# Heads of a gated DeltaNet layer in one encoder kernel: separate streams for values, scans and outputs, SiLU on ScalarE, z multiplied in during the first gate

## Chip, cores, metric

One core of a Trainium2 chip runs the whole layer. The metric is the device time of one execution in microseconds (us), the median of several runs. TensorE (PE), VectorE (DVE), ScalarE (ACT), GpSimd (POOL) and SyncE (SP, which issues the DMAs here) each work through their own queue in order.

## The reference

One encoder layer over 1024 tokens and 16 meta tokens of 1024 channels, in float32. The change touches the branch with the gated delta rule and its neighbour:

```python
h = rmsnorm(h_res, norm1_w[l])
proj = h @ w_in[l]     # q k v z beta a | sc_b sc_c sc_x | gate_a gate_b
...
qkv = silu(depthwise_conv_centred(concatenate([q, k, v]), conv_w))     # 5 taps
qc = l2norm(qc) * DN_DK ** -0.5;  kc = l2norm(kc)
o_fwd = chunk_gated_delta_rule(qp, kp, vp, gp[:, :, 0], bp[:, :, 0])
o_bwd = flip(chunk_gated_delta_rule(flip(qp), flip(kp), flip(vp), ...))
o = o_fwd + o_bwd
o = o * rsqrt(mean(o * o) + RMS_EPS) * norm_w
o = o * silu(z)
...
y_a = o_dn @ w_branch_dn
y_b = (sc_b * depthwise_conv_centred(sc_c * sc_x, sc_conv_w)) @ w_branch_sc
merged = sigmoid(gate_a) * y_a + sigmoid(gate_b) * y_b
h_res = h_res + merged @ w_out
```

A SwiGLU block and a final norm follow. There are 8 heads of 128 channels; `depthwise_conv_centred` on `sc_c * sc_x` has 3 taps.

## The kernel before

Activations lie with channels on the partitions. Every float32 operand of a large matmul is split into a high and a low fp32r part, and a product is three matmuls (high x high, high x low, low x high).

**The stage of heads** (lines 200 to 1333) takes nearly half of the time. Its order is not left to the scheduler: a planner in Python emits the instructions of all engines one by one and keeps a clock `T` for each engine, advanced by estimates: `pe(ns)` for TensorE, `V(n)` for VectorE, `A(n)` or `on("act", ns)` for ScalarE. TensorE's backbone are dense units, 128 output channels each, 48 or 72 matmuls: q, k and v of each head (`u_qkv`, L366), z (`u_z`, L453), and C, x and B of the short conv (`u_short`, L417). Between two steps of a dense unit, `run_streams` (L978) resumes every stream (a generator) whose yielded time has come, and `pump` (L300) gives VectorE the next instruction of a lane: `conv`, `short`, `fs` or `norm`, the ready lane with the least weighted time spent (`WEIGHT`, L265).

The streams: `g_decay` (L508) fetches the decay rows of a head, masks them and takes their exponentials; `g_norm` (L536) makes norms and the products of keys and queries; `g_meta` (L631) does the meta tokens; `g_inv` (L649) inverts the triangular blocks, by `fs_job` on VectorE for blocks of 32 and by matmuls up to 128; `g_scan` (L751) turns the values round (L764 to 771), waits for the inverse, runs 8 steps forward and backward at once (L796 to 881), and then norms, scales, turns and stores the output (L884 to 911). In its last step it fetches z of the head (L819), which L908 multiplies in. `lock["scan"]` lets one of the inverse's matmul part and the scan at a time use the three PSUM banks of `pss()` (L67); dense units have three (`psm`, L61), `g_norm` has two (`psd`, L64).

SiLU is written as x (1 + tanh(x/2)) / 2: the factors 0.5 are in the conv weights (L1125) and the output weight (L1127), ScalarE takes the tanh (L359, L463), and VectorE multiplies (L362, L467). `half_buffer` (L344) gives the temporaries of these, of the short conv and of its products, three of them.

**The border.** Behind the stage its pools are closed (L1333) and new ones opened in the same memory. The last B unit (channels 896 to 1023 of the short conv) is loaded and multiplied there (L1437 to 1445), with `front` (L1431) loading the first operands A, E, C and so on of the next stage in between. From there on the scheduler orders the instructions. The next stage are four products of 1024 x 1024 by Strassen-Winograd, seven part products A to G each (`seven`, L1375): gate b, gate a, the short-conv branch, the DeltaNet branch. `during_gb` (L1475) lists what is put between the steps of gate b's seven products, mainly loads for gate a. The DeltaNet branch reads `o_d`, the heads' outputs in DRAM (L1541).

Of the kernel before, what the change touches and what calls it, by code (L numbers as in the profile page):

```python
# [24 lines left out]
H = 8  # L25
# [11 lines left out]
def encoder_layer(ctx: ExitStack, tc: tile.TileContext, x, meta, norm1_w, w_in,  # L37
# [29 lines left out]
    def pss():  # L67
        return ps.tile([P, 512], F32, tag="d", name=uid("pd"), bufs=3)
# [3 lines left out]
    def psany():  # L72
        rot["i"] += 1
        return (psm, psm, psm, psd, psd, pss, pss, pss)[rot["i"] % 8]()
# [137 lines left out]
    ARRIVE = 5000  # L212
    LAND = 5500
# [51 lines left out]
    WEIGHT = {"conv": 1.0, "short": 1.0, "fs": 0.33, "norm": 0.1}  # L265
# [78 lines left out]
    def half_buffer():  # L344
        return d1.tile([P, 520], F32, tag="rb", name=uid("rb"), bufs=3)

    def conv_job(raw, dst, col, st_, first):

        for h0, hn in ((first, 520 - first), HALF[1]):
# [8 lines left out]
            th = half_buffer()  # L358
            nc.scalar.activation(th[:, :hn], acc, AF.Tanh)  # L359
            on("act", 0, T["dve"] + HOP)  # L360
            yield A(hn)
            nc.vector.scalar_tensor_tensor(out=acc, in0=th[:, :hn], scalar=1.0, in1=acc, op0=ALU.add, op1=ALU.mult)  # L362
            t = V(hn, 1)
# [37 lines left out]
    def short_job(cx, j, ycs):  # L401
        for i in range(2):
            yc = half_buffer()
            ycs.append(yc)
            nc.vector.tensor_scalar(out=yc[:, :512], in0=cx[:, 1 + 512 * i:513 + 512 * i], scalar1=cols[:, j:j + 1],
                                    scalar2=None, op0=ALU.mult)
            V(512, 2)
            yield T["dve"] + DEP
# [8 lines left out]
    def u_short(j, i, w):  # L417
# [22 lines left out]
        else:  # L440
            force(st_["job"])
            ycs = [half_buffer()[:, :512] for _ in range(2)]
# [10 lines left out]
    def u_z(h, w):  # L453

        rest = None
        for i in range(2):
            po = psm()
            for k, _ in enumerate(dense_steps(po, w, hx, META + 512 * i, 512)):
                if k == 3 and rest:
                    rest()  # L460
                yield
            th = half_buffer()[:, :512]
            nc.scalar.activation(th, po, AF.Tanh, scale=0.5)  # L463
            A(512)

            def rest(i=i, th=th, po=po):
                nc.vector.scalar_tensor_tensor(out=th, in0=th, scalar=1.0, in1=po, op0=ALU.add, op1=ALU.mult)  # L467
                V(512)
                nc.sync.dma_start(z_d[h][:, 512 * i:512 * i + 512], th)
        T["dve"] = max(T["dve"], T["act"] + HOP)  # L470
        rest()
# [36 lines left out]
    def g_decay(h, st_):  # L508
# [8 lines left out]

        arrived = []
        for i in range(NC + 1):
            while i < NC and h > 1 and heads[h - 2]["steps"] <= i:  # L520
                yield T["pe"] + 100
            if i < NC:
                arrived.append(fetch(i))
            for k in ((i - 1,) if i < NC else (NC - 1,)):
                if k < 0:
                    continue
                yield arrived[k]
                nc.vector.tensor_tensor(out=PQ[:, k], in0=PQ[:, k], in1=mask2, op=ALU.add)  # L528
                yield V(256)
                for d, c in enumerate((k, NC - 1 - k)):  # L530
                    hd = d * 8 + h
                    nc.scalar.activation(PQ[:, k, d], PQ[:, k, d], AF.Exp, bias=negG2[:, c, hd:hd + 1])  # L532
                    st_["exp"][c, d] = on("act", 295)
                yield T["act"]

    def g_norm(h, st_):  # L536
# [3 lines left out]
        small = dn.tile([P, 9, 12], F32, tag="small", name=uid("small"), bufs=3)  # L540
        st_["small"] = small
        ssk, ssq, rk2, ssk1, y, _, sk = (small[:, :, i] for i in range(7))
        cc, ce = small[:, :, 7:9], small[:, :, 9:11]
# [105 lines left out]
    def g_inv(h, st_):  # L649

        NP = st_["NP"]
        E = dn.tile([P, 2, NC, 32], F32, tag="T2", name=uid("E"))
# [10 lines left out]
        for b in range(4):  # L663
            nc.scalar.copy(E[B(b)].rearrange("p d c i -> p c d i"), NP[B(b), :, :, B(b)])
            A(512)
# [23 lines left out]
        T2 = dn.tile([P, 2, NC, 32], F32, tag="T2", name=uid("T2"))[:, 0]  # L689
        rows_, turned_ = (W, Z), (Z, W)  # L690

        def diag(d, b):
            nc.scalar.copy(NP[B(b), :, d, B(b)], rows_[d][B(b), d])
            A(256)
# [635 lines left out]
    for g in rest:  # L1330
        for _ in g:
            pass
# [617 lines left out]
```

## Time and profile before

| | us |
|---|---|
| median of 3 runs | 1993.39 (1990.38 to 1996.84) |
| profiled execution | 1995.63 |
| its span, first to last instruction | 1993.9 |

Busy shares of the span, from the page: TensorE 98%, VectorE 74%, ScalarE 47%, GpSimd 9%. Stages in the profiled execution: the inputs are normed and turned round up to about 50 us; the stage of heads lasts to 941 us; the four branch products to about 1260 us; the output projection and the SwiGLU block to the end.

A row of busy times by stretch gives the stretch, its length, busy time and number of instructions of each engine, TensorE's granted clock (1.00 is full), the DMA engines' busy share and GB/s. A row of a group gives line, engine, operation, output and inputs, shapes, count, then busy time, mean ns of one, idle time before them and what ended it. A row of waits gives who waited for whom: total us, times, longest. A row of DMA issues ends with the median us from issue to landing. In a timeline row stand start and length in us. `pm`, `pe` and `pd` are the PSUM tiles of `psm`, `psd` and `pss`; `SPq` is SyncE issuing a DMA.

### The profile page before, as it was taken

The page shows a single profiled execution, that of the slowest core. Times are in us where ns is not written, and L with a number is a line of the kernel's source. Part 1 is how long each engine was busy: PE and PEld are TensorE (multiplying, and loading weights), DVE is VectorE, ACT ScalarE, POOL GpSimd, SP SyncE. Part 2 cuts the span into 40 slices and gives each one's busy share as a digit, 9 for nine tenths or more (in the row PEclk, how much of TensorE's full clock was granted, in tenths as well). Part 3 has the DMA queues.
Part 4 walks back from the last instruction along what each step waited for, and adds up shares of the span by engine and source line. Part 5 has one row for each costly group of instructions (what it writes and reads, how often), then busy time and mean ns, then how long its engine had stood idle before and what let it go on. Part 6 is the DMA issues. An engine that isn't in the chain of part 4 may idle for free.

```text
span 1993.9 us, 32160 instructions
## 1 busy us (share of the span) xinstructions
PE 1945.6 (98%) x11914; PEld 1700.9 (85%) x11914; DVE 1479.4 (74%) x2812; ACT 937.0 (47%) x2142; POOL 173.5 (9%) x497
## 2 busy tenths in 40 slices
PE   9999999999999999998999999999999999999998
PEld 8998899898989899987788788887888888888887
DVE  4788768788878788866656888758887977856574
ACT  5465475746475646342445555234323322324343
POOL 2132012123012022100000000000000000000001
PEclk9999999999999999999999999999999999999999
DMA  4123231212222112254864732332575645487654
GB/s 143 53 62 86 77 89 38 80 42 68 59 70 52 57 49 70 70 166 151 322 226 144 263 127 84 118 121 68 191 237 201 227 152 185 154 282 247 190 181 160
DMA packets 218226, 267.37 MB, mean 134 GB/s; under 512 B 14756, under 2 KB 133957, under 8 KB 216661
## 3 DMA queue, kind: packets, MB, share of 16 engines
q1 hardware_dynamic: 218069, 265.33, 41.0%
q8 instruction: 93, 1.52, 0.3%
q14 instruction: 64, 0.52, 0.1%
HBM read 192.84 MB, written 72.43 MB: 133 GB/s over the span
## 4 chain that ended last, share of the span: by engine, by line
PE 58%; DVE 4%; ACT 2%; DMA 1%; issue 1%; POOL 0%; POOLq 0%; SPq 0%; ACTq 0%; DVEq 0%
PE pm L331 6%; PE pm L1390 5%; PE pd L1390 5%; PE pe L1390 4%; PE pm L1676 3%; PE pm L1677 3%; PE pm L1675 3%; PE pd L1675 2%; PE pd L1677 2%; PE pd L1676 2%; PE pe L1675 2%; PE pe L1676 2%; PE pe L1677 2%; PE pm L1833 1%; PE pm L1834 1%; PE pm L1832 1%
## 5 line engine op out<-in xcount | busy, mean ns | idle before, releaser
L331 PE MATMUL pm<-hTh,wh 128*128 128x384 f32 (+4 forms) x1200 | 433.9, 363 | 0.1
L331 PE MATMUL pm<-hTh,wl 128*128 128x384 f32 (+4 forms) x1200 | 402.2, 336 | 0.0
L331 PE MATMUL pm<-al,wh 128*128 128x384 f32 (+4 forms) x1200 | 401.0, 335 | 0.5 <-DVE al L1057 0.5
L331 PEld LDWEIGHTS pm<-hTh,wh 128*128 128x128 f32 x1200 | 227.1, 190 | 9.2 <-ACT hTh L1051 0.2
L331 PEld LDWEIGHTS pm<-hTh,wl 128*128 128x128 f32 x1200 | 226.1, 189 | 10.3
L331 PEld LDWEIGHTS pm<-al,wh 128*128 128x128 f32 x1200 | 227.3, 190 | 8.4 <-DVE al L1057 0.7
L86 DVE TENSOR_TENSOR al<-raw,ring_h 128x1024 fp32r<-128x1024 f32 x73 | 88.4, 1222 | 64.3 <-ACT ring_h L85 64.1
L85 ACT CAST ring_h<-raw 128x1024 fp32r<-128x1024 f32 x73 | 77.0, 1055 | 109.7 <-PE pd L1834 38.0
L947 DVE TENSOR_TENSOR wl<-raw,wh 128x512 fp32r<-128x512 f32 x106 | 72.5, 685 | 43.2 <-ACT wh L950 43.0
L354 DVE SCALAR_TENSOR_TENSOR kq<-ra,wc,kq 128x520 f32<-128x520 f32 (+1 forms) x128 | 95.7, 748 | 1.5
L85 ACT CAST raw<-pair 128x1024 fp32r<-128x1024 f32 (+1 forms) x56 | 53.8, 961 | 86.7 <-PE pd L1390 34.9
L127 POOL TENSOR_SCALAR ss<-ss 128x1 f32<-128x1 f32 x13 | 4.5, 349 | 1015.5 <-ACT b L1844 602.5
L86 DVE TENSOR_TENSOR wl<-pair,wh 128x1024 fp32r<-128x1024 f32 (+1 forms) x56 | 61.9, 1106 | 39.5 <-ACT wh L85 39.4
L86 DVE TENSOR_TENSOR raw<-pair,raw 128x1024 fp32r<-128x1024 f32 (+1 forms) x56 | 61.9, 1105 | 29.8 <-ACT raw L85 27.8
L85 ACT CAST wh<-pair 128x1024 fp32r<-128x1024 f32 (+1 forms) x56 | 53.8, 960 | 61.0 <-PE pe L1390 29.0
L828 ACT ACTIVATE w<-pd,small 128x128 f32<-128x128 f32 x128 | 40.0, 364 | 88.6 <-PE pd L821 72.8
L485 DVE TENSOR_TENSOR tm<-fP,fN 128x126 f32<-128x126 f32 (+22 forms) x248 | 62.9, 254 | 6.9
L489 DVE TENSOR_TENSOR fP<-fP,tm 128x126 f32<-128x126 f32 (+22 forms) x248 | 62.7, 253 | 6.7
L950 ACT CAST wh<-raw 128x512 fp32r<-128x512 f32 x106 | 65.2, 619 | 0.1
L1345 DVE TENSOR_TENSOR b<-pm,b 128x512 f32<-128x512 f32 x65 | 43.6, 684 | 21.7 <-PE pm L1677 19.0
L85 ACT CAST mB<-raw 128x1024 fp32r<-128x1024 f32 x24 | 25.1, 1052 | 69.8 <-DVE raw L140 53.6
L532 ACT ACTIVATE PQ<-PQ,negG 128x128 f32<-128x128 f32 x128 | 44.2, 394 | 26.4 <-DVE PQ L528 26.1
(646 smaller groups left out, 5243.6 us busy)
## 6 DMA issues: line engine op xcount, KB each, us to landing
raw<-in_w_in_dram SPq DMA_DIRECT2D x56, 512.0 KB, 4.5
raw<-in_w_gate_up_dram SPq DMA_DIRECT2D x44, 512.0 KB, 5.2
sums<-in_w_down_dram SPq DMA_DIRECT2D x22, 512.0 KB, 4.9
t_d<-sums SPq DMA_DIRECT2D x11, 1024.0 KB, 3.9
raw<-s_d SPq DMA_DIRECT2D x44, 256.0 KB, 3.4
raw<-t_d SPq DMA_DIRECT2D x44, 256.0 KB, 3.6
act_d<-b SPq DMA_DIRECT2D x43, 256.0 KB, 2.7
pair<-in_w_in_dram SPq DMA_DIRECT2D x10, 1024.0 KB, 9.8
```

What stands on the lines that cost most here:

```text
L85: nc.scalar.copy(hi, src)
L86: nc.vector.tensor_tensor(out=lo, in0=src, in1=hi.bitcast(F32), op=ALU.subtract)
L331: mm(po[:, :n], (wl if j == 2 else wh)[:, k], xl[k][:, t0:t0 + n] if j == 1 else xh[k][:, t0:t0 + n], start=(i == 0), stop=(i == 3 * KT - 1))
L354: nc.vector.scalar_tensor_tensor(out=acc, in0=raw[:, h0 + t:h0 + t + hn], scalar=wc[:, t, col:col + 1], in1=acc, op0=ALU.mult, op1=ALU.add)
L485: nc.vector.tensor_tensor(out=tv, in0=fP[:, 0:r, j:j + 1].broadcast_to([P, r, n]), in1=fN[:, j:j + 1, j + 1:32].broadcast_to([P, r, n]), o ...
L489: nc.vector.tensor_tensor(out=fP[:, 0:r, j + 1:32], in0=fP[:, 0:r, j + 1:32], in1=tv, op=ALU.subtract)
L947: nc.vector.tensor_tensor(out=u[1][1][:, k], in0=u[2][:, k], in1=u[1][0][:, k].bitcast(F32), op=ALU.subtract)
L950: nc.scalar.copy(u[1][0][:, k], u[2][:, k])
L1390: mm(bank[t], a[:, c], b, start=fresh, stop=first and k == 3 and j == 2, skip_group_check=not first)
L1675: mm(po, ah[:, k], bhk, start=k == 0, stop=False)
L1676: mm(po, ah[:, k], blk, start=False, stop=False)
L1677: mm(po, al[:, k], bhk, start=False, stop=k == 3)
```

## The change

- `g_scan` is divided: `g_vals` turns round the values, in three groups, each as soon as the scan before is past the chunks that it overwrites (`vS` is one tile for all heads now); `g_scan` holds the steps alone and no lock; `g_out` norms, scales, turns and stores. A scan starts when values, inverse and meta part are there; each kind is a stream of its own.
- PSUM: `pss` has two banks, for the scan alone; a new `psv` has one, shared under the lock by values, inverse and outputs. The inverse takes `E` and `px` from the dense banks.
- SiLU is an activation: in place in the convs, on z straight from PSUM; the factors 0.5 go. The first tap of the short conv and the output's weight go from VectorE to ScalarE.
- z is no longer multiplied in by the scan. `times_z` loads `o_d` and `z_d` of a head, multiplies and stores `o_d`, once per head in gate b's products B to E, with one buffer `w2`.
- `g_decay` takes the exponentials in batches (all 8 chunks for heads 0 and 1, else 6 and 2), and the planner counts a `LOAD` of 1283 ns on each side. Other estimates change (415, 375, 628 ns), and the weight of the lane `fs` goes from 0.33 to 4.0.
- Buffers: one `half_buffer` and one `conv_buffer` in place of three; two of `o`.
- Border: the last B unit's weights are loaded and split in the stage (`cover`), and `front`'s first entry (A and E) is issued ahead of `yc`.

```diff
     def pss():
-        return ps.tile([P, 512], F32, tag="d", name=uid("pd"), bufs=3)
+        return ps.tile([P, 512], F32, tag="d", name=uid("pd"), bufs=2)
+
+    def psv():
+        return ps.tile([P, 512], F32, tag="v", name=uid("pv"), bufs=1)
...
-    WEIGHT = {"conv": 1.0, "short": 1.0, "fs": 0.33, "norm": 0.1}
+    WEIGHT = {"conv": 1.0, "short": 1.0, "fs": 4.0, "norm": 0.1}
...
     def half_buffer():
-        return d1.tile([P, 520], F32, tag="rb", name=uid("rb"), bufs=3)
+        return d1.tile([P, 512], F32, tag="rb", name=uid("rb"), bufs=1)
+
+    def conv_buffer():
+        return d1.tile([P, 512], F32, tag="yb", name=uid("yb"), bufs=1)
...
-            th = half_buffer()
-            nc.scalar.activation(th[:, :hn], acc, AF.Tanh)
+            nc.scalar.activation(acc, acc, AF.Silu)
             on("act", 0, T["dve"] + HOP)
-            yield A(hn)
-            nc.vector.scalar_tensor_tensor(out=acc, in0=th[:, :hn], scalar=1.0, in1=acc, op0=ALU.add, op1=ALU.mult)
-            t = V(hn, 1)
+            t = A(hn)
...
         for i in range(2):
-            yc = half_buffer()
+            yc = conv_buffer()
             ycs.append(yc)
-            nc.vector.tensor_scalar(out=yc[:, :512], in0=cx[:, 1 + 512 * i:513 + 512 * i], scalar1=cols[:, j:j + 1],
-                                    scalar2=None, op0=ALU.mult)
-            V(512, 2)
-            yield T["dve"] + DEP
+            nc.scalar.activation(yc[:, :512], cx[:, 1 + 512 * i:513 + 512 * i], AF.Copy, scale=cols[:, j:j + 1])
+            yield A(512)
...
             th = half_buffer()[:, :512]
-            nc.scalar.activation(th, po, AF.Tanh, scale=0.5)
+            nc.scalar.activation(th, po, AF.Silu)
             A(512)
-
-            def rest(i=i, th=th, po=po):
-                nc.vector.scalar_tensor_tensor(out=th, in0=th, scalar=1.0, in1=po, op0=ALU.add, op1=ALU.mult)
-                V(512)
-                nc.sync.dma_start(z_d[h][:, 512 * i:512 * i + 512], th)
+            nc.sync.dma_start(z_d[h][:, 512 * i:512 * i + 512], th)
...
+        for i0, i1 in ((0, 6), (6, 8)) if h > 1 else ((0, 8),):
+            for i in range(i0, i1):
+                while h > 1 and heads[h - 2]["steps"] <= i:
+                    yield T["pe"] + 100
                 arrived.append(fetch(i))
+                if i - 2 >= i0:
+                    masked(i - 2)
+            for i in (i1 - 2, i1 - 1):
+                yield arrived[i]
+                masked(i)
+            yield T["dve"] + HOP
+            on("act", LOAD)
+            for i in range(i0, i1):
+                for d, c in enumerate((i, NC - 1 - i)):
                     hd = d * 8 + h
+                    nc.scalar.activation(PQ[:, i, d], PQ[:, i, d], AF.Exp, bias=negG2[:, c, hd:hd + 1])
                     st_["exp"][c, d] = on("act", 295)
+            on("act", LOAD)
+            yield T["act"]
...
+    def g_vals(h, st_):
+
+        vT, sk = st_["vT"], st_["small"][:, :, 5]
+        for grp, free in (((8, 3, 4), 5), ((2, 5, 1), 7), ((6, 0, 7), 8)):
+            while h and heads[h - 1].get("steps", 0) < free:
+                yield T["pe"] + 100
+            yield from take("vals")
+            pt = vbank()
             for i, c in enumerate(grp):
                 transpose(pt[:, i], vT[:, 0:P] if c == 8 else vT[:, cs(c)])
             yield pe(330)
             for i, c in enumerate(grp):
                 nc.scalar.activation(vS[:, c], pt[:, i], AF.Copy, scale=sk[:, c:c + 1])
                 A(P)
+            lock["scan"] = None
+            yield T["act"] + HOP
...
+    def g_out(h, st_):
...
             yield t
+            yield from take("out")
+            pt = vbank()
             for c in range(4):
                 transpose(pt[:, c], oacc[4 * c4 + c])
             yield pe(430)
-            nc.vector.scalar_tensor_tensor(out=oT, in0=pt, scalar=cols[:, 24:25], in1=zT[:, 4 * c4:4 * c4 + 4],
-                                           op0=ALU.mult, op1=ALU.mult)
-            V(512, 1)
+            nc.scalar.activation(oT, pt, AF.Copy, scale=cols[:, 24:25])
+            t = A(512)
+            lock["scan"] = None
...
-        if h < H and not scans and heads[h].get("sk") and "tv" in heads[h] and heads[h]["tv"]():
-            scans.append([g_scan(h, heads[h]), T["dve"] + HOP, h])
+        if h < H and not scans and all(heads[h].get(k) for k in ("inverted", "learned", "valued")):
+            scans.append([g_scan(h, heads[h]), T["pe"], h])
...
-            for q in (scans, invs, metas, norms, decs):
+            for q in (scans, vals, invs, metas, outs, norms, decs):
...
-    w = wload(w_in, OSB + 7 * P)
+    front.pop(0)()
     yc = s4(SEQ)
     nc.sync.dma_start(yc, yc_d[7])
     for i in range(2):
         po = psany()
-        dense(po, w, hx, C0 + META + 512 * i, 512)
+        dense(po, cover[1], hx, C0 + META + 512 * i, 512)
...
+    def times_z(j):
+        o_ = big("w2", [P, D], F32)
+        nc.sync.dma_start(o_, o_d[j])
+        for h_ in halves:
+            z_ = tp.tile([P, 512], F32, tag="t2", name=uid("t2"), bufs=2)
+            nc.sync.dma_start(z_, z_d[j][:, h_])
+            nc.vector.tensor_tensor(out=o_[:, h_], in0=o_[:, h_], in1=z_, op=ALU.mult)
+        nc.sync.dma_start(o_d[j], o_)
...
+    for j in range(H):
+        during_gb[1 + j // 2][2 + 2 * (j % 2)].append(lambda j=j: times_z(j))
```

More of the change, by code (lines that the diff above doesn't have):

```diff
@@ L212, in encoder_layer @@
     ARRIVE = 5000
+    LOAD = 1283
     LAND = 5500
@@ L771, in g_scan, with newbank @@
                 A(P)
-        lock["scan"] = None
-        yield T["act"] + HOP - 1000
-        while not (st_.get("inverted") and st_.get("learned")):
-            yield T["pe"] + 100
-        yield from take("scan")
+            lock["scan"] = None
+            yield T["act"] + HOP
+    def g_scan(h, st_):
+        nonlocal freed, near
+        kq, small, kn, NP, PQ = (st_[k] for k in ("kq", "small", "kn", "NP", "PQ"))
+        kT, qT = kq[:, 0], kq[:, 1]
+        cc, ce = small[:, :, 6:8], small[:, :, 8:10]
+        sso = small[:, :, 10]
+        st_["steps"] = 0
+        def newbank():
+            return pss().rearrange("p (a n) -> p a n", a=4)
         Pm = st_["Pm"]
-        O = dn.tile([P, NC, P], F32, tag="o", name=uid("o"))
+        O = st_["O"] = dn.tile([P, NC, P], F32, tag="o", name=uid("o"), bufs=2)
         oacc = [O[:, c] for c in range(NC)]
@@ L881, in g_scan @@
             yield t
+    def g_out(h, st_):
+        nonlocal scaled_heads
+        small, O = st_["small"], st_["O"]
+        ssq, y, sso = (small[:, :, i] for i in (1, 4, 10))
+        oacc = [O[:, c] for c in range(NC)]
         def norm():
@@ L890, in norm @@
             yield T["dve"] + DEP
-        lock["scan"] = None
         yield T["act"] + HOP
@@ L976, in start_streams @@
                 rest.append(block_sums())
+        h = nout
+        if h < H and not outs and heads[h].get("scanned"):
+            outs.append([g_out(h, heads[h]), T["pe"], h])
+            nout += 1
     def run_streams():
@@ L988, in run_streams @@
                         h = q.pop(0)[2]
-                        if q is scans:
-                            done += 1
-                        elif q is not decs:
-                            heads[h]["inverted" if q is invs else "learned" if q is metas else "normed"] = True
+                        done += q is outs
+                        for q_, what in ((scans, "scanned"), (vals, "valued"), (invs, "inverted"), (metas, "learned"), (norms, "normed")):
+                            if q is q_:
+                                heads[h][what] = True
                     else:
@@ L1037, in turned @@
             for g in range(2):
-                bank = banks[t, g] = (psd() if g and t < 2 else pss()).rearrange("p (k t) -> p k t", k=4)
+                third = psd if g and t < 2 else (pss, pss, psv)[turns["i"] % 3]
+                turns["i"] += third is not psd
+                bank = banks[t, g] = third().rearrange("p (k t) -> p k t", k=4)
                 for k in range(4):
@@ L1332, in encoder_layer @@
             pass
+    for k in range(cover[3][0], 4):
+        split_part(cover, k)
     ph1.close()
```

108 lines of the change are left out of this document (43 added, 65 removed).

## The prediction

> **What bounds the kernel now.** I read the page first, then the busy times by stretch, then TensorE's waits in the stage of heads, then the border behind that stage in order of time.
>
> ```profile
> span 1993.9 us, 32160 instructions
> PE 1945.6 (98%) x11914; PEld 1700.9 (85%) x11914; DVE 1479.4 (74%) x2812; ACT 937.0 (47%) x2142; POOL 173.5 (9%) x497
> core 0: us, PE busy (x) PEld busy (x) DVE busy (x) ACT busy (x) POOL busy (x), PEclk, DMA share, GB/s
> 50.00:900.00 850.00, 825.00 (x6787) 769.71 (x6786) 668.05 (x1768) 488.35 (x1516) 142.14 (x432) 1.00 0.25 71
> 941.40:949.90 8.50, 0.03 (x1) 0.01 (x1) 1.33 (x3) 0.69 (x2) 0.00 (x0) 0.75 0.82 294
> 949.90:956.00 6.10, 6.07 (x15) 4.76 (x16) 6.10 (x8) 1.49 (x3) 0.00 (x0) 0.51 1.05 390
> 956.00:1110.00 154.00, 152.76 (x670) 124.93 (x669) 99.75 (x106) 79.76 (x112) 0.00 (x0) 1.00 0.65 228
> 1110.00:1950.00 840.00, 838.99 (x3733) 693.95 (x3732) 629.08 (x808) 308.40 (x378) 7.40 (x16) 1.00 0.53 177
> ```
>
> TensorE bounds it: 98% busy, and from 956 to 1950 only 1.24 + 1.01 us are idle. The change takes away no matmul, so it can win only where TensorE stands or runs slowly: 25.0 us idle in the stage of heads (850 minus 825.00), 8.5 us at the border, and behind the border 6.1 us at a granted clock of 0.51, worth 6.1 x 0.49 = 3.0 us. That is 36.5 us in all, 1.8% of the time; small gaps after a change from small to large matmuls are not counted and stay.
>
> ```profile
> PE pe L588 <- DVE PQ L626: 8.2, 6, 2.8
> PE pd L821 <- DVE r L813: 4.2, 5, 1.2
> PE pe L82 <- DVE Nm L571: 2.9, 4, 1.4
> PE pe L82 <- ACT jk L550: 2.5, 2, 2.3
> PE pd L710 <- ACT T L704: 2.0, 2, 1.3
> PE pd L699 <- DVE W L684: 1.6, 3, 0.9
> ```
>
> These are TensorE's waits between 50 and 900 us (total, times, longest). VectorE ends 16.9 us of these 21.4. No single wait is longer than 2.8 us: the planner's order is nearly right, and what is left are many short stalls, mostly where VectorE (668 of 850 us, 79%) is late.
>
> ```profile
> 939.03 1.46 SPq L911 DMA_DIRECT2D o_d<-o  x2
> 940.82 0.39 PE L119 MATMUL pm<-al,wh 128*128 128x512 f32 x1
> 941.04 0.39 PE L120 MATMUL pm<-hTh,wl 128*128 128x512 f32 x1
> 942.25 0.32 SPq L1439 DMA_DIRECT2D s<-yc_d  x1
> 942.62 2.78 SPq L1354 DMA_DIRECT2D pair<-in_w_in_dram  x4
> 949.21 0.62 ACT L85 CAST raw<-pair 128x512 fp32r<-128x512 f32 x1 [10.36 <-DMA pair<-in_w_in_dram]
> 949.93 0.77 PE L1390 MATMUL pm<-hTh,raw 128*128 128x512 f32 x1 [8.50 <-ACT raw L85]
> ```
>
> At the border the last output leaves at 939.03, the new pools' first transfers start at 942.25 behind it, the first block lands 6.6 us after its issue (942.62 to 949.21), and TensorE has run out of work at 941.
>
> **The change part by part.**
>
> *Border.* The last short-conv unit (48 matmuls of 512 columns, one per 0.22 us by the two rows at 940.82 and 941.04: 10.6 us) is no longer loaded behind the stage; its weights are split in it. The loads of A and E go ahead of that of yc. In before this unit already ran, but between the last steps of the last scan. How much comes back depends on who ends the stage. If head 7's output does, as now, little changes: A no longer queues behind the load of yc (942.25 to 942.62, 0.4 us). If dense units end it, the unit's 10.6 us lie over the 6.6 us of the load, and idle time and slow clock go: 11.5 us.
>
> ```profile
> L784 PE MATMUL pd<-vS,meta_inv x16: 270/273/275, 206.1 to 875.4; 128*128 128x128 f32 x16
> L885 DVE TENSOR_SCALAR small<-small x8: 151/164/168, 273.2 to 933.7; 128x9 f32<-128x9 f32 x8
> ```
>
> L784 opens each of the 8 scans and L885 follows it: a scan starts every (875.4 - 206.1)/7 = 95.6 us and lasts 58 us (875.4 to 933.7) to 67 us (206.1 to 273.2). About a third of the cycle no scan runs, because the inverse takes the lock only after the scan has let go of it. With own banks for the scan, inverse h+1 can lie beside scan h, the heads finish earlier, and dense work is left for the end. I take 9 of 11.5 us, ends 0 and 11.5.
>
> *VectorE to ScalarE.*
>
> ```profile
> L362 DVE SCALAR_TENSOR_TENSOR kq<-rb,kq 128x520 f32<-128x520 f32 (+1 forms) x32 | 22.1, 690 | 9.4 <-ACT rb L359 9.4
> L362 DVE SCALAR_TENSOR_TENSOR vT<-rb,vT 128x520 f32<-128x520 f32 x16 | 11.2, 698 | 8.9 <-ACT rb L359 8.8
> L467 DVE SCALAR_TENSOR_TENSOR rb<-rb,pm 128x512 f32<-128x512 f32 x16 | 10.9, 678 | 5.2 <-ACT rb L463 5.1
> L405 DVE TENSOR_SCALAR rb<-ra,cols 128x512 f32<-128x512 f32 x16 | 7.7, 480 | 3.3 <-DMA p_d<-rb 3.3
> L908 DVE SCALAR_TENSOR_TENSOR o<-pd,cols,vS 128x512 f32<-128x512 f32 x16 | 11.9, 742 | 7.9 <-PE pd L82 7.7
> L463 ACT ACTIVATE rb<-pm 128x512 f32<-128x512 f32 x16 | 9.5, 593 | 13.4 <-PE pm L331 13.3
> L532 ACT ACTIVATE PQ<-PQ,negG 128x128 f32<-128x128 f32 x128 | 44.2, 394 | 26.4 <-DVE PQ L528 26.1
> L1690 ACT ACTIVATE b<-b x21: 626/634/635, 1364.3 to 1764.9; 128x512 f32<-128x512 f32 x21
> L1690 ACT ACT_TABLE_LOAD  x1: 1283/1283/1283, 1363.0 to 1363.0; - x1
> ```
>
> All five VectorE groups go from the stage: 22.1 + 11.2 + 10.9 + 7.7 + 11.9 = 63.8 us, so VectorE falls from 79% to 71%. ScalarE keeps its activations (SiLU in place of tanh) and gains 16 short-conv products and 16 outputs, 32 x 0.593 = 19 us. It also gains table loads: SiLU needed one at L1690, where tanh, exp, square and copy had run without. Each batch of exponentials now stands between two loads: 2 batches for heads 0 and 1, 2 x 6 for the others, 14 x 2 x 1.283 = 36 us, and a few at the gates. ScalarE goes from 488 to about 545 us of 850, 64%: room on average. I take 10 of the 25.0 us of waits as won, ends 0 and 22 (the small waits on the first rows do not all belong to VectorE's load).
>
> By the Trainium skill, "ScalarE: Activation LUTs", section "What ACT_TABLE_LOAD costs", a switch costs 1.28 us of load and 1.38 us of drain, which speaks against this part. The load in this trace is 1.283 us, and the skill's drain does not show there: L1690 loads at 1363.0 and activates at 1364.3. With the drain the 28 loads would be an estimated 39 us dearer, still hidden on average.
>
> *What the bursts cost.* ScalarE is taken for 16 x 0.394 + 2 x 1.283 = 8.9 us at a stretch for heads 0 and 1, 7.3 us (12 exponentials) and 4.1 us (4) for the others. Behind a burst stand the copies out of the dense banks, the halves of the next weights and the scan's w and v2. The three dense banks give two chunks of time; a chunk is 24 matmuls of 347 columns on average (1040 in three chunks), so 2 x 24 x 0.22 x 347/512 = 7 us, less when the inverse borrows one for E or px. The trace has no such burst, so bounds: 0, if all fits; 14 x 2 us = 28 us, if each burst overruns by 2.
>
> ```profile
> yc_d<-rb SPq DMA_DIRECT2D x16, 256.0 KB, 2.2
> SPq L515 <- PE pd L841: 251.2, 45, 13.8
> ```
>
> The buffers shrink too: one conv buffer for both halves of a short-conv row makes ScalarE, in order, wait for the first half's store before it starts the second, 0.3 + 2.2 us, 8 times, 20 us of standing ScalarE, more where the SP queue waits for a scan (the second row). The scan has two banks in place of three: its second bank is rewritten (L806) right after L803, so the output adds of the step before (L875) are now due then. I take 5 us for bursts, buffers and banks together, ends 0 and 48; nearest to nothing, since the average load stays under two thirds.
>
> *z later.* 8 calls times_z in products B to E of the first gate: each loads 1 MB, multiplies twice 0.68 us (as L467), stores 0.5 MB; the fetch of z in the scan goes (0.5 MB each).
>
> ```profile
> pair<-in_w_in_dram SPq DMA_DIRECT2D x10, 1024.0 KB, 9.8
> pair<-o_d SPq DMA_DIRECT2D x4, 256.0 KB, 2.8
> tb_d<-s SPq DMA_DIRECT2D x16, 256.0 KB, 2.2
> 942.00:975.00 33.00, 25.07 (x98) 20.48 (x99) 20.27 (x23) 10.89 (x17) 0.00 (x0) 0.84 0.95 350
> 975.00:1000.00 25.00, 25.00 (x112) 20.67 (x112) 17.08 (x17) 15.35 (x21) 0.00 (x0) 1.00 0.67 231
> ```
>
> VectorE has room for 10.9 us more (17.08 of 25). DMA is full (0.95) until 975, and behind it a third is free. I take 1 us, ends 0 and 57 (worked out as the third rival).
>
> *Sum* against the profiled execution, 1995.6 us (span 1993.9): - 9 - 10 + 5 + 1 = -13, 1982.6. The median of the runs, 1993.4, lies 2.2 us under the profiled one, so 1980 us.
>
> **The rivals.**
>
> 1. *The scans no longer wait, and TensorE is full.* Inverses beside scans let dense work run unbroken at the end. For it: the 95.6 us cycle around a 60 us scan. Against: TensorE works now through the whole cycle, so there is nothing to win but the 25.0 us. Border 11.5 and 20 of the waits, costs 2: 1993.4 - 29.5 = 1964.
>
> 2. *It does not do what it says: the waits change owner.* The short stalls come from an order fixed ahead that no planner gets quite right, now with ScalarE in bursts. Border 9, waits 10, costs 17: 1993.4 - 2 = 1991.
>
> 3. *Slower, through times_z's one buffer.* The loads of call j+1 wait until call j is stored, and the multiply stands in VectorE's queue ahead of the operand splits and the sums that TensorE waits for. A cycle is load, 2 x 0.68, store: with the rows of small transfers 2.8 + 1.4 + 2.2 = 6.4 us, with the crowded 1 MB row 9.8 + 1.4 + 2.2 = 13.4. The calls lie two to a product, 48 x 0.22 = 10.6 us, so 8 calls have 42 us and some three operand steps of lead, 8 us; it decides from (42 + 8)/8 = 6.3 us a cycle. At 13.4 it costs 107 - 50 = 57 us, at a middle 9.5 us 26. Against it: if the scheduler puts the multiplies late in VectorE's queue, nothing waits, since o_d is not read before the last branch. With 26 us on the forecast: 2006.
>
> **How the numbers follow.** Forecast 1980 (1972 to 1988): 0.42. Rival 1, 1964: 0.20. Rival 2, 1991: 0.20. Rival 3, 2006 and beyond: 0.18. About 0.3% (6 us) can be told from no change: faster 0.60, same 0.22, slower 0.18. The range from 1955 (all of 36.5 us and a little) to 2006 leaves out the further part of rival 3 and little else.
>
> **What would show it.** Border: TensorE's gap between its last dense matmul and the first at L1390 under 2 us, granted clock there near 1.00. VectorE: about 604 us between 50 and 900, and the waits of L588 and L821 on it halved. ScalarE: some 30 table loads of 1.283 us, and TensorE's new waits, if any, with ScalarE or a dense bank as releaser. Scan banks: waits of L806 on L875. times_z: no wait of L1390 on VectorE, no VectorE wait for o_d or z. The forecast is wrong if the idle time of the stage stays at 25 us or more, if head 7's output still ends the stage, or if TensorE stands in the first gate.

## The result, and the profile after

The changed kernel takes 2010.75 us (median of 4 runs, 2005.81 to 2011.42), the kernel before, beside it, 1993.99 (1990.38 to 1996.84): a ratio of 1.008, 95% interval 1.0057 to 1.0103. It is slower; 1980 us with a range of 1955 to 2006 was forecast, so the time lies outside the range, on the wrong side. The profiled execution took 2011.1 us, its span 2009.4 against 1993.9.

First the page of the changed kernel:

```profile
span 2009.4 us, 32113 instructions
PE 1951.0 (97%) x11914; PEld 1707.5 (85%) x11914; DVE 1423.4 (71%) x2733; ACT 984.2 (49%) x2198; POOL 164.7 (8%) x497
```

Then its busy times by stretch (columns as before):

```profile
50.00:900.00 850.00, 809.44 (x6734) 760.14 (x6734) 618.96 (x1705) 541.04 (x1598) 132.89 (x432) 0.98 0.22 63
...
900.00:950.00 50.00, 50.00 (x227) 41.41 (x226) 13.20 (x25) 9.61 (x23) 2.18 (x1) 1.00 0.46 151
950.00:1000.00 50.00, 50.00 (x222) 41.20 (x221) 30.59 (x34) 20.25 (x29) 0.00 (x0) 1.00 0.81 296
1000.00:1050.00 50.00, 49.47 (x219) 40.63 (x218) 33.17 (x42) 24.13 (x37) 0.00 (x0) 1.00 0.92 313
1050.00:1100.00 50.00, 50.00 (x222) 41.42 (x221) 28.60 (x33) 24.71 (x35) 0.00 (x0) 1.00 0.93 325
1100.00:1150.00 50.00, 45.64 (x189) 35.97 (x189) 42.91 (x45) 24.45 (x30) 0.00 (x0) 0.97 0.78 271
```

Three stages tell three stories. The border is clean: no idle time and full clock from 900 to 1000, where before had 8.5 us idle and 6.1 us at clock 0.51. The stage of heads is worse: 40.6 us idle (850 minus 809.44) against 25.0, and a granted clock of 0.98 against 1.00. And the first gates, between 1100 and 1150, now stand 4.4 us, behind DMA engines at 0.92 and 0.93.

How much each is worth shows one group of matmuls that both kernels have in the branch products, first and last start. The first row is of the kernel before, the second of the changed one:

```profile
L1390 PE MATMUL pm<-raw,raw x132: 389/389/390, 974.8 to 1245.5; 128*128 128x512 f32 x132
```

```profile
L1413 PE MATMUL pm<-raw,raw x132: 387/389/497, 984.3 to 1260.7; 128*128 128x512 f32 x132
```

By their first start 984.3 - 974.8 = 9.5 us are lost, by their last 15.2: so the branch products lose 5.7 us. With the border's 11.5 us won (8.5 + 3.0, the prediction's own count), the stage of heads must have lost some 21 us (9.5 + 11.5).

TensorE's waits in the changed kernel between 50 and 900 us (total, times, longest):

```profile
PE pe L587 <- DVE PQ L625: 15.1, 9, 2.9
PE pe L587 <- DVE fP L481: 9.2, 3, 3.6
PE pd L822 <- DVE r L817: 4.6, 2, 2.7
```

The second of these rows in the kernel before (the first stands in the prediction):

```profile
PE pe L588 <- DVE fP L489: 0.7, 1, 0.7
```

VectorE's waits between 50 and 850, first of the kernel before, then of the changed one:

```profile
DVE wl L947 <- ACT wh L950: 37.4, 27, 7.8
```

```profile
DVE wl L955 <- ACT wh L958: 65.7, 28, 10.9
...
DVE vT L361 <- ACT vT L392: 13.4, 9, 3.0
DVE kq L361 <- ACT kq L392: 13.0, 10, 2.1
```

L587 (L588 before) multiplies keys and queries into the two `psd` banks, and VectorE reads them out (L619, L625). The waits of L588 on VectorE were to be halved; they went from 8.9 us (8.2 + 0.7) to 24.3 (15.1 + 9.2), with VectorE 49 us less busy; those of L821 (now L822) stayed, 4.2 and 4.6. VectorE is late because it stands, mostly in front of L955, which subtracts the high part of the next weights once ScalarE has rounded it (L958), and also in front of L361, the taps of the convolution that add to the one ScalarE makes (L392). Ten waits at L587 are longer than 1 us: in the trace five of them, 14.6 us, follow a stand of VectorE at L955, four, 7.6 us, one at L361. One place of the changed kernel in order of time shows how (start, length, idle time before and its releaser):

```profile
355.20 1.28 ACT L530 ACT_TABLE_LOAD   x1
...
356.49 3.62 ACT L530 ACTIVATE PQ<-PQ,negG 128x128 f32<-128x128 f32 x12
...
360.02 0.60 ACT L958 CAST wh<-raw 128x512 fp32r<-128x512 f32 x1
...
360.66 0.69 DVE L955 TENSOR_TENSOR wl<-raw,wh 128x512 fp32r<-128x512 f32 x1 [4.66 <-ACT wh L958]
...
363.56 0.60 DVE L619 SCALAR_TENSOR_TENSOR NP<-pe,small,PQ 128x128 f32<-128x128 f32 x2
...
364.38 0.41 DVE L625 TENSOR_TENSOR PQ<-pe,PQ 128x256 f32<-128x256 f32 x1
...
364.94 0.87 PE L587 MATMUL pe<-kq 128*128 128x256 f32 x2 [3.63 <-DVE fP L481]
```

A load and twelve exponentials hold ScalarE for 4.9 us. The high part waits behind them; VectorE, whose queue is in order, stands 4.66 us in front of the low part; the reads of the banks stand behind that; and TensorE, out of work at 361.3, goes on at 364.94, after 3.63 us. The releaser named in the last row is another instruction of the same late queue; what frees the bank is L625.

The wait is paid for twice. The same place of the changed kernel, by stretch:

```profile
361.00:365.00 4.00, 0.37 (x4) 0.13 (x2) 3.72 (x16) 3.27 (x9) 0.42 (x2) 1.00 0.00 0
365.00:368.00 3.00, 3.00 (x13) 2.89 (x13) 2.63 (x6) 0.00 (x0) 2.24 (x9) 0.55 0.02 5
368.00:371.00 3.00, 2.32 (x73) 1.96 (x71) 2.82 (x11) 2.34 (x9) 1.26 (x3) 0.88 0.27 43
```

After the 3.63 us TensorE is busy, but at a granted clock of 0.55 for 3 us, then 0.88: 3 x 0.45 + 3 x 0.12 = 1.7 us more.

### The profile page after: what moved, and what is told of

Same layout as the page of the kernel before. It is cut to its first block, busy times and chain, and to the rows that moved or that the text cites. A ratio compares the mean times of both kernels' runs of the same rounds, so it can differ in the third digit from the quotient of the medians.

```text
span 2009.4 us, 32113 instructions
## 1 busy us (share of the span) xinstructions
PE 1951.0 (97%) x11914; PEld 1707.5 (85%) x11914; DVE 1423.4 (71%) x2733; ACT 984.2 (49%) x2198; POOL 164.7 (8%) x497
## 4 chain that ended last, share of the span: by engine, by line
PE 79%; DVE 8%; ACT 7%; DMA 4%; issue 2%; SPq 0%; POOL 0%; POOLq 0%; DVEq 0%; ACTq 0%
PE pm L335 24%; PE pm L1413 4%; PE pm L1710 3%; PE pe L1413 3%; PE pm L1711 3%; PE pm L1709 2%; PE pd L1413 2%; PE pe L1710 2%; PE pd L1710 2%; PE pe L1711 2%; PE pe L1709 2%; PE pd L1709 2%; PE pd L1711 2%; PE pm L1868 1%; PE pm L1867 1%
## 5 line engine op out<-in xcount | busy, mean ns | idle before, releaser
L955 DVE TENSOR_TENSOR wl<-raw,wh 128x512 fp32r<-128x512 f32 x108 | 74.0, 686 | 77.8 <-ACT wh L958 77.6
L361 DVE SCALAR_TENSOR_TENSOR kq<-ra,wc,kq 128x520 f32<-128x520 f32 (+1 forms) x128 | 95.7, 748 | 14.4 <-ACT kq L392 13.0
L958 ACT CAST wh<-raw 128x512 fp32r<-128x512 f32 x108 | 66.4, 619 | 23.5 <-PE pm L335 23.3
L132 POOL TENSOR_TENSOR small<-small,minus_half 128x9 f32<-128x9 f32 x16 | 30.6, 1910 | 406.0 <-DVE small L592 255.7
L587 PE MATMUL pe<-kq 128*128 128x256 f32 x128 | 38.7, 403 | 24.3 <-DVE PQ L625 15.1
L1368 DVE TENSOR_TENSOR b<-pm,b 128x512 f32<-128x512 f32 x65 | 43.6, 684 | 24.6 <-PE pm L1711 22.2
```

What stands on the lines that cost most here:

```text
L361: nc.vector.scalar_tensor_tensor(out=acc, in0=raw[:, h0 + t:h0 + t + hn], scalar=wc[:, t, col:col + 1], in1=acc, op0=ALU.mult, op1=ALU.add)
L955: nc.vector.tensor_tensor(out=u[1][1][:, k], in0=u[2][:, k], in1=u[1][0][:, k].bitcast(F32), op=ALU.subtract)
L958: nc.scalar.copy(u[1][0][:, k], u[2][:, k])
```

## The experiments

Five theories were tested: **A**, the transfers of `times_z` cost the gates some 5 us. **B**, ScalarE in bursts makes VectorE stand at the weights' low part, and TensorE pays. **C**, the rival: streams, banks and overlap of inverse and scan are at fault, and a repair at the low part only reshuffles the waits. **D**, the border was forecast right. **E**, the weight of the `fs` lane. Changes in us are between medians, against the changed kernel unless another run is named; "before" was run again with each group of experiments, at 1994.3 to 1995.2.

**1. No `times_z`** (z is not multiplied in).

```diff
-    for j in range(H):
-        during_gb[1 + j // 2][2 + 2 * (j % 2)].append(lambda j=j: times_z(j))
```

> Leaves out the multiplication by silu(z) (the eight calls of times_z with their loads and stores). Theory A (the 4 MB of extra transfers keep the DMA engines at .92 in 1000 to 1100 and so the pieces of in_w and the first products of the gates come late): 4 to 7 us less than the changed kernel, about 2005 us, and no wait of PE over 1 us behind an input weight in 1050 to 1150. Rival (the weights would be late there anyway, since cover and border were moved): within 2 us of the changed kernel, with that wait of PE still there. The stage of heads (50 to 900) must look as in the changed kernel in both cases: about 40 us of idle PE.

2005.64 us, 5.1 less; the ratio to before is 1.0056 (1.0041 to 1.0071). TensorE's wait behind an input weight goes, and DMA shares fall to 0.70 and 0.49 between 1000 and 1100; the stage of heads is as before this edit. Theory A holds.

**2. High parts first, low parts when due.**

```diff
+        i = (0, 2, 1, 3)[i]
...
-            if ahead[0] and n_ in SPL:
-                split_part(ahead[0], SPL.index(n_))
+            if ahead[0]:
+                i_ = ahead[0][3][0]
+                if i_ < 4 and n_ >= SPL[i_] and (i_ < 2 or max(T["pe"], T["dve"]) >= ahead[0][3][i_ - 1]):
+                    split_part(ahead[0], i_)
```

(`split_part` also records in `ahead[0][3]` when the planner takes a high part for ready.)

> Only the order changes: both parts of the high weights are issued on ScalarE first, and the parts that VectorE subtracts are issued only once the planner takes the high part for ready. Theory B (a batch of exponentials holds ScalarE some 5 us, VectorE stands in front of the subtraction behind it, and the copies of the kkq banks queue behind that): VectorE's waits for the high part fall from 65.7 us to under 30 in 50 to 850, PE's idle time in 50 to 900 from 40.6 to about 30, the time by 8 to 12 us to about 2000 us. Theory C (what is lost is lost at the split of the streams and the banks, which this doesn't touch): VectorE's waits for the high part fall too, but others of VectorE grow instead, and the time stays within 3 us of the changed kernel.

1998.27 us, 12.5 less. VectorE's waits for the high part fall from 65.7 to 3.6 us; others grow (for L807 15.9 to 26.3), as C has it, but the time falls as B has it, and TensorE is idle 33.8 us in place of 40.6. VectorE still stands behind ScalarE's bursts, now at the tap, and TensorE's waits at L587 fall only to 13.1 us:

```profile
268.85 0.76 DVE L361 SCALAR_TENSOR_TENSOR vT<-ra,wc,vT 128x520 f32<-128x520 f32 x1 [4.61 <-ACT vT L392]
...
270.09 1.20 PE L587 MATMUL pe<-kq 128*128 128x256 f32 x2 [4.56 <-DVE PQ L625]
```

**3 and 4. No table loads; then no batches either** (tanh in place of SiLU in the stage of heads, so z, q, k and v differ from the reference's).

```diff
-    LOAD = 1283
+    LOAD = 0
...
-            nc.scalar.activation(acc, acc, AF.Silu)
+            nc.scalar.activation(acc, acc, AF.Tanh)
...
-            nc.scalar.activation(th, po, AF.Silu)
+            nc.scalar.activation(th, po, AF.Tanh)
```

The second one also has the loop of the kernel before in `g_decay`: two exponentials at a time.

> Computes tanh where the stage of heads computes SiLU (convolutions and z), so that ScalarE loads no table there, and the planner counts none; the exponentials stay in their batches. Theory B1 (the loads make the burst): PE's idle time in 50 to 900 falls from 40.6 to about 28, the time by 10 to 15 us to about 1998. Theory B2 (the twelve exponentials together make it: 3.6 us of them against 1.3 us of load): a fall of 2 to 6 us, to about 2006. Theory C (split and banks): within 3 us of the changed kernel.

> As the kernel with tanh in place of SiLU in the stage of heads, and the exponentials are issued two at a time between other work, as in the kernel before, not in batches of twelve and four. Theory B1: as with the batches, about 1998 us. Theory B2: PE's idle time in 50 to 900 falls to about 25, the time by 12 to 18 us to about 1995. Theory C: still within 3 us of the changed kernel, with VectorE's waits for the high part back at about 37 us and PE's waits for the kkq banks nevertheless over 15 us.

2001.85 us, 8.9 less, and 1993.64 us, 17.1 less. So loads and batches cost about alike, 8.9 and 8.2 us. Both sizes of B were partly right, and C is out as the only cause. TensorE's waits for VectorE at L587 fall to 3.0 us and then 1.4 (L580 there), though VectorE still stands some 41 us in front of the low part in both. But even the second only equals before, although the border is won and VectorE has 46 us less to do: something is left, of which `times_z` is some 5 us.

**5. The border alone**, in the kernel before.

```diff
+    fill_units.append((OSB + 7 * P, None, None, None))
...
-    w = wload(w_in, OSB + 7 * P)
+    front.pop(0)()
     yc = s4(SEQ)
...
-        dense(po, w, hx, C0 + META + 512 * i, 512)
+        dense(po, cover[1], hx, C0 + META + 512 * i, 512)
```

> The kernel before with the border of the change alone: the eighth cover's weights are loaded and split in the stage of heads, and the first entry of front is issued ahead of yc. Theory D (the border was forecast right, and the loss is all in the stage and the gates): 9 to 13 us less than before, 1981 to 1986 us, no gap of PE over 2 us in 935 to 960, VectorE's waits and PE's 25 us of idle time in 50 to 900 as before. Rival (in the kernel before the last head's scan and output end the stage, so a cover split early has nothing to hide and the slow clock stays): at most 3 us less, 1991 us or more.

1992.14 us, ratio 0.9991 (0.9983 to 1.0000): theory D falls, the rival holds. SyncE's queue of this kernel, then TensorE at the border:

```profile
936.32 1.47 SPq L911 DMA_DIRECT2D o_d<-o  x2
939.53 0.93 SPq L1360 DMA_DIRECT2D pair<-in_w_in_dram  x2
...
945.59 0.77 PE L1396 MATMUL pm<-hTh,raw 128*128 128x512 f32 x1 [7.09 <-ACT raw L85]
```

The first weights of the gates are issued behind the store of head 7's output, as before, and land as late. The gap of 8.5 us shrinks to 7.1. What freed the border in the changed kernel is the earlier end of the heads. Its scans open with the first row, its outputs are stored with the second; the third is the store of the kernel before:

```profile
L788 PE MATMUL pd<-vS,meta_inv x16: 270/275/275, 217.6 to 836.3; 128*128 128x128 f32 x16
...
L917 SPq DMA_DIRECT2D o_d<-o x16: 319/320/376, 300.8 to 914.7; - x16
...
L911 SPq DMA_DIRECT2D o_d<-o x16: 319/320/381, 281.0 to 940.2; - x16
```

A scan starts every (836.3 - 217.6)/7 = 88.4 us in place of 95.6, the last output leaves at 914.7 in place of 940.2, and dense units end the stage.

**6. As 4, with the order of 2.**

> As the kernel with tanh in place of SiLU and the exponentials spread out, and both high parts of the weights are issued first, VectorE's subtractions once the high part is taken for ready. Theory B (the 41 us that VectorE still stands in front of the subtraction there pass through to PE): 5 to 8 us less than that kernel, 1986 to 1989 us, PE's idle time in 50 to 900 under 20. Theory C (a plan is only reshuffled; other waits grow): within 3 us of it, PE's idle time still about 25.

1973.03 us, ratio 0.9896 (0.9882 to 0.991): 20.6 less than 4, where 5 to 8 were expected. Its stage by stretch:

```profile
50.00:900.00 850.00, 836.54 (x6895) 783.55 (x6894) 622.64 (x1721) 518.97 (x1594) 144.69 (x433) 1.00 0.25 70
```

TensorE is idle 13.5 us, and the clock is whole. This is what was left in 4: the low part at the head of VectorE's queue costs more than batches or loads alone. Against the changed kernel the two repairs together give 37.7 us, more than the 17.1 of 4 and the 12.5 of 2 added up.

**7. As 4, the weight of `fs` as before the change.**

```diff
-    WEIGHT = {"conv": 1.0, "short": 1.0, "fs": 4.0, "norm": 0.1}
+    WEIGHT = {"conv": 1.0, "short": 1.0, "fs": 0.33, "norm": 0.1}
```

> As the kernel with tanh in place of SiLU and the exponentials spread out, with the weight of the fs jobs back at 0.33. Theory E (at weight 4.0 the fs jobs go to VectorE ahead of the copies that free banks): 3 to 7 us less than that kernel, 1987 to 1991 us. Rival (the weight decides nothing): within 3 us of it, 1991 to 1997 us; at the low weight the inverse may also start later, which would show as PE waits for fP.

2003.61 us, 10.0 more than 4. Theory E falls: the new weight helps.

**8. As 2, z multiplied in where the DeltaNet branch reads `o_d`**, on GpSimd.

```diff
             nc.sync.dma_start(dn_[key][:, k, hi], o_d[4 * kh + k][:, halves[half]])
+        w_ = big("w2", [P, 2, 512], F32)
+        zs = [w_[:, 0], w_[:, 1]] + [tp.tile([P, 512], F32, tag="t2", name=uid("t2"), bufs=2) for _ in range(2)]
+        for k in range(4):
+            nc.sync.dma_start(zs[k], z_d[4 * kh + k][:, halves[half]])
+        for k in range(4):
+            x_ = dn_[key][:, k, hi]
+            nc.gpsimd.tensor_tensor(out=x_, in0=x_, in1=zs[k], op=ALU.mult)
```

> The kernel with the weights' high parts first, and without times_z: z is multiplied in where the last product's blocks of o are read, 16 pieces on GpSimd, so o is neither read nor written once more (4 MB of transfers in place of 12). Theory A (the transfers of times_z cost the gates 5 us, and GpSimd is idle where it now multiplies): 4 to 6 us less than with the high parts first alone, about 1993 us, DMA share at most .7 in 1000 to 1100. Rival (GpSimd's multiplications come late and the sums of the last product's blocks wait for them): the time stays at 1998 us or above, with VectorE or PE waiting for a pair behind GpSimd in 1100 to 1250.

2004.31 us, 6.0 more than 2. The gates are rid of their wait (DMA share 0.68 and 0.48 between 1000 and 1100), but a new one appears in the branch behind them:

```profile
1150.00:1200.00 50.00, 44.68 (x185) 36.37 (x184) 44.97 (x48) 18.55 (x21) 6.97 (x4) 0.93 0.42 138
```

TensorE stands 5.3 us between 1150 and 1200, with VectorE busy 45 of 50 us; VectorE waited 2.8 us for a weight of the DeltaNet branch. The DMA share between 1100 and 1150 is 0.82, against 0.76 in 2. A multiplication takes GpSimd 1.8 to 2.0 us, against 0.68 on VectorE. How much is GpSimd's slowness and how much the transfers' new place was not told apart.

**9. The order of 2 alone, in the kernel before.**

> The kernel before with nothing but the order of the weights' parts changed: both high parts first on ScalarE, VectorE's subtractions once the high part is taken for ready. Theory B (VectorE standing in front of that subtraction is a loss of every version of this stage, 37 us of it in the kernel before): 6 to 12 us less than before, 1982 to 1988 us, PE's idle time in 50 to 900 under 20. Rival (it only matters where scans, inverses and outputs may run apart, as in the change): within 3 us of before, PE's idle time about 25.

1985.74 us, ratio 0.9955 (0.9939 to 0.9972), 9.5 less. VectorE's waits for the high part fall from 37.4 to 2.6 us, TensorE's idle time in the stage from 25.0 to 20.3, and the gap at the border from 8.5 to 3.6, since the heads end earlier here too. So the loss is older than the change. By VectorE's waits (37.4 and 65.7 us) the change made it larger; the gains, 9.5 and 12.5 us, lie too close to show that.

**10 and 11. SiLU from tanh as before, exponentials spread, the order of 2; then z in the output, too.** Nothing is left out. The tanh goes into the row buffer that the taps have read already:

```diff
-            nc.scalar.activation(acc, acc, AF.Silu)
+            th = raw[:, h0:h0 + hn]
+            nc.scalar.activation(th, acc, AF.Tanh)
...
+            nc.vector.scalar_tensor_tensor(out=acc, in0=th, scalar=1.0, in1=acc, op0=ALU.add, op1=ALU.mult)
```

and for 11, in `g_out`:

```diff
+        zT = st_["kn"][:, 0:NC]
+        nc.sync.dma_start(zT, z_d[h].rearrange("p (c t) -> p c t", c=NC))
...
-            nc.scalar.activation(oT, pt, AF.Copy, scale=cols[:, 24:25])
+            nc.vector.scalar_tensor_tensor(out=oT, in0=pt, scalar=cols[:, 24:25], in1=zT[:, 4 * c4:4 * c4 + 4],
+                                           op0=ALU.mult, op1=ALU.mult)
```

> The change with SiLU computed from tanh as in the kernel before (a tanh on ScalarE into the row buffer already read, then one operation of VectorE: 64 more of about 0.69 us, 44 us more of VectorE in 50 to 900), exponentials spread out, high parts of the weights first. Nothing is left out. Theory B (what the change lost was VectorE standing behind ScalarE, and 44 us more of work without a wait find room in 850): within 8 us of the kernel that leaves the 64 operations out, 1973 to 1981 us, and 14 to 21 us less than before. Rival (VectorE's added work delays the banks as much as the waits did): 1988 us or more.

> As the kernel of the row above, with z multiplied in by VectorE where the output of a head leaves its bank, as before the change, z loaded into the head's own kn tile; times_z and its 12 MB of transfers go. Theory A: 4 to 6 us less than the row above through the gates (no wait of PE over 1 us behind an input weight in 1000 to 1150), about 1970 to 1976 us. Rival (16 multiplications more on VectorE in the stage, with the values' bank held for them, give it back): within 2 us of the row above or slower, with more of PE's idle time in 50 to 900.

1981.71 us, ratio 0.9936 (0.9921 to 0.995), and 1982.69 us. The first is 29.0 us under the changed kernel and beats both. VectorE is busy 661 us in its stage, 43 more than in the changed kernel, and TensorE is idle 19.9 us: load was not the trouble. In 11 the gates are clean, but one wait of 8.1 us appears in the inverse, up to 836.8, and takes the gain back. It begins with ScalarE, which stands in front of the one conv buffer until that is stored, with the inverse's copies behind it:

```profile
827.35 0.72 ACT L412 ACTIVATE yb<-ra,cols 128x512 f32<-128x512 f32 x1 [6.37 <-DMA yc_d<-yb]
831.76 0.72 ACT L412 ACTIVATE yb<-ra,cols 128x512 f32<-128x512 f32 x1 [3.69 <-DMA yc_d<-yb]
```

The stretches around it:

```profile
830.00:835.00 5.00, 0.00 (x0) 0.00 (x0) 2.32 (x4) 3.19 (x9) 0.00 (x0) 0.69 0.15 57
835.00:840.00 5.00, 3.22 (x35) 2.94 (x36) 1.92 (x4) 4.63 (x13) 0.00 (x0) 0.50 0.62 198
840.00:845.00 5.00, 5.00 (x45) 3.87 (x45) 0.00 (x0) 1.44 (x4) 0.00 (x0) 0.79 0.03 11
```

The clock is 0.50 and 0.79 after it.

**12. The changed kernel with the order of 2 and z in the output**, SiLU and batches kept.

> The change with SiLU and batches as it has them, high parts of the weights first, and z multiplied in by VectorE where the output leaves its bank; times_z goes. Theory A and B together: 4 to 6 us less than with the high parts first alone (1998.3), 1992 to 1995 us, about as before. Rival: 1998 us or more, with the gates' wait gone and more of PE's idle time in 50 to 900.

1984.95 us, ratio 0.9947 (0.9932 to 0.9962), 13.3 less than 2 where 4 to 6 were expected: in the stage, too, TensorE is idle 24.5 us in place of 33.8. Why more than the gates' share came back is open; the outputs left ScalarE for VectorE, and the plan is another.

**13 and 14. How far plans scatter**: one estimate moved that is not in dispute, in the changed kernel and in the kernel before.

```diff
-    HOP, TOPE, DEP = 200, 370, 127
+    HOP, TOPE, DEP = 210, 370, 127
```

> The changed kernel with one planner number moved that no theory speaks of: HOP, the time from one engine's result to the next engine's start, 200 to 210 ns. Nothing of the work changes, only which of two nearly equal steps is issued first. If plans of one kind scatter little: within 3 us of the changed kernel, 2008 to 2014 us. If they scatter as widely as the repairs moved the time: 5 us or more away to either side.

> The kernel before with the same number moved, 200 to 210 ns. Little scatter: within 3 us of before, 1991 to 1998 us. Wide scatter: 5 us or more away, and then a change of 9.5 us by the order of the weights' parts in that kernel could be chance.

2006.88 us, 3.9 less, and 1990.49 us, 4.5 less than the before beside it. A plan can be better or worse by 4 to 5 us without any change of the work; with one such move in each kernel, how much wider the scatter may be isn't known. Against these two the 12.5, 20.6 and 10.0 us of 2, 6 and 7 stand, 17.1 for 4 stands, its halves of 8.9 and 8.2 are rough, and of the 9.5 us of 9 nearly half could be luck.

**15. The order 0, 2, 1, 3 alone**, without waiting for the high part, in the changed kernel.

```diff
+        i = (0, 2, 1, 3)[i]
```

> The changed kernel with both high parts issued first and VectorE's subtractions third and fourth, at the same four steps as ever, without waiting for the planner's time of the high part. If the order does it (two steps of the dense unit more, some 0.5 us, between the high part and its subtraction): 8 to 13 us less than the changed kernel, about 2000 us, with VectorE's waits in front of the subtraction under 35 us. If the waiting does it (behind a batch ScalarE is 5 us late, far more than two steps): at most 4 us less, and most of the 65.7 us of those waits still there.

2006.14 us, 4.6 less, no more than scatter, though VectorE's waits there fall from 65.7 to 15.7 us, which neither side expected. So the size of VectorE's waits alone doesn't foretell the gain. TensorE now stands elsewhere, as C has it: in front of the one bank `psv`, which the inverse (L698) can take only when ScalarE has copied the values out of it (L765). In three of these four waits, 15.0 us, ScalarE has twelve exponentials in front of that copy, so a batch reaches TensorE without VectorE, too. First the row of this run, then that of run 2:

```profile
PE pv L698 <- ACT vS L765: 16.3, 4, 5.3
```

```profile
PE pv L698 <- ACT vS L765: 6.6, 2, 4.6
```

Run 2, which also waits for the planner's time, is 7.9 us faster than run 15; this is more than the scatter seen, if not by much. That the waiting is what acts is likely and not shown.

**16. SiLU, exponentials spread, the order of 2.**

> The changed kernel with SiLU, the high parts first, and the exponentials spread out two at a time, so that ScalarE loads a table whenever it goes from a SiLU to an exponential and back (the planner counts none). With some 64 pairs of exponentials and 64 SiLUs between them I expect 60 to 100 loads of 1.28 us, 80 to 130 us more of ScalarE where it is busy 541 of 850. If a load anywhere costs about what it takes from ScalarE's slack: near the version with batches and high parts first, 1990 to 2000 us. If scattered loads hurt more than batches: 2005 us or more, with PE's idle time in 50 to 900 over 45.

2018.92 us, ratio 1.0123 (1.0108 to 1.0138); TensorE is idle 44.6 us in the stage, where over 45 was the sign. Its table loads:

```profile
L524 ACT ACT_TABLE_LOAD x34 | 43.6, 1283 | 0.6
L365 ACT ACT_TABLE_LOAD x30 | 38.5, 1283 | 2.0 <-DVE kq L361 1.3 <-DVE vT L361 0.3
L461 ACT ACT_TABLE_LOAD x9 | 11.5, 1283 | 4.4 <-PE pm L335 3.5 <-issue 0.8
```

73 loads, 93.6 us (43.6 + 38.5 + 11.5). Batches, whose loads the planner counts, are the lesser evil where SiLU and the exponential share a stage: 20.7 us less (2). Spread loads that the planner counts were not tried. Neither is needed where tanh stands for SiLU (10).

## Why the prediction was wrong

**Border, -9.** Right in size (11.5 us came back), and the condition named there decided it: dense units end the stage, not head 7's output. The moved cover by itself gave some 2 us (run 5), which is less than the scatter; the rest came with the earlier end of the heads. That this is due to the split streams alone isn't shown: in run 9, without them, the gap shrank to 3.6 us, too. The step that the scans would start sooner was right: 88.4 us against 95.6.

**VectorE to ScalarE, -10, and bursts, buffers and banks, +5.** This is where the forecast failed. The work moved as worked out: VectorE fell from 668 to 619 us (604 were forecast; between 50 and 950, which holds all of the heads' work, it fell by 67, where 64 were worked out), ScalarE rose from 488 to 541 (545), 28 us of it by 13 + 9 table loads in convolutions and exponentials. The burst itself was even sized too long: 7.3 us for twelve exponentials with two loads, where 4.9 were measured with one load.

But "room on average" was taken for room at the moment. The failed step is "nearest to nothing, since the average load stays under two thirds". The prediction priced a burst by what stands behind it on ScalarE and by the dense banks' lead of 7 us. It did not go one queue further: the low part of the next weights stands in VectorE's queue behind the high part in ScalarE's, and behind it everything that VectorE owes to TensorE, the reads of the two `psd` banks first, where TensorE stood 24.3 us. New waits were looked for with ScalarE or a dense bank as releaser; most of those that came name VectorE. The forecast for the two terms was -5; they cost some 21. The prediction's bound of 28 us for bursts, 2 us for each of 14, would have covered it; the value taken did not.

Run 4 gives 17.1 us to loads and batches, run 2 12.5 to the place of the low part with loads and batches kept, and run 6 37.7 to both. This is more than was lost, since the kernel before had part of the second loss already (run 9). Buffers and banks were little trouble in the changed kernel: TensorE's waits at L810 (L806 before) for the output adds come to 1.1 us in all, those for the bank `psv` to 3.8, and ScalarE stood 8.3 us in front of the one conv buffer, where 20 were counted. They come forward in the repaired versions: `psv` with 16.3 us in run 15, and the 8.1 us of run 11 begin at the conv buffer.

Each us of waiting was priced too low as well: the slow clock was counted at the border and not in the stage, where the granted clock fell from 1.00 to 0.98. Of the 21 us, 15.6 are idle time; some 5 are left for the clock.

**times_z, +1.** The mechanism was the third rival's, the size not: 5.1 us (run 1), between the 1 us taken and the rival's 26. The rows of the changed kernel: VectorE stood 12.2 us in front of the multiplication (longest 3.8), SyncE 24.6 in front of the loads of z; the first gates' weights came late once, for 2.8 us. "Behind it a third is free" held for the engines' share, but 12 MB filled that third to 0.93.

**The rivals.** The second one named the cause ("now with ScalarE in bursts") and gave it 1991, with the waits still 10 us fewer; they became 15.6 more. Its sentence that the waits change owner came true where a repair was made (runs 11 and 15). That the idle time of the stage could rise was written down only as what would refute the forecast.

The Trainium skill, "ScalarE: Activation LUTs", "What ACT_TABLE_LOAD costs", adds a drain to the load; here, too, the trace shows none: the load at 355.20 took 1.28 us and the exponentials began at 356.49. For the slow clock, the Trainium skill's "TensorE: Matmul & The Clock Gate", Part 1, says that the array falls to half clock after an idle window of some 3.4 us and comes back after a busy one of that length. The 0.55 after 3.63 us and 0.50 after 8.1 us agree. Half of one such window is an estimated 1.7 us, as after the 3.63 us; the border of the kernel before, 6.1 us at 0.51, lost more, 3.0.

## What to carry over

Follow a burst one queue further than the engine that has it: who stands in order behind the instruction that waits for it, and what does that engine owe to the bottleneck? An instruction whose input comes from another engine is best issued when that input is due, not when its turn comes; a few lines of the planner to that end won 9.5 us before the change, nearly half of which could be luck, and 12.5 after; the order alone, without waiting, won no more than scatter. And before crediting a part of a change with a gain, move an estimate that stands for nothing: here two plans of the same work differ by 4 to 5 us.

## What was not expected

Waits of TensorE of 3.6 and 8.1 us are followed by 6 to 8 us at a granted clock of 0.50 to 0.88, in the midst of a stage that is 95% busy. The table loads show the bare 1.283 us in all groups of run 16. And GpSimd takes 1.8 to 2.0 us for a product of 128x512 that VectorE does in 0.68.
